# One core's diffusion layer: the last scan ahead of the early output projection, two blocks gathered in PSUM beside the norms, and the last five combinations in the rings of the others

## The chip, the core and the metric

The kernel runs on one core of one Trainium2 chip. Its work is done by TensorE (PE in the rows: matmuls; PEld is its loading of weights), VectorE (DVE), ScalarE (ACT) and GpSimd (POOL); SyncE (SP) issues most transfers. The metric is the device time of one execution in microseconds (us). The time before is the median of three runs. One more execution was recorded by the hardware profiler; its span runs from the first to the last recorded instruction.

## The reference

One layer of a diffusion backbone over 512 latent tokens of width 1024 with a context of 256. A token mixer (two groups of gated linear recurrences, four heads each, scanned in both directions), one output projection, a norm, and then a retrieval of experts:

```python
def reference(x, c, ctx, c_ctx, w_ada, ...):
    ...
    u_l = modulate(x, sh1_l, sc1_l) @ w_in[i]
    u_c = modulate(xc, sh1_c, sc1_c) @ w_in[i]
    mix_c, mix_l = token_mixer(u_c, u_l, rows, ...)
    x = layer_norm(ALPHA * x + g1_l * (mix_l @ w_out[i]), ln_gamma[i, 0], ln_beta[i, 0])
    ...
    y_l = peer(modulate(x, sh2_l, sc2_l), peer_w_query[i], peer_sub_keys[i], peer_u[i], peer_v[i])
    x = layer_norm(ALPHA * x + g2_l * y_l, ln_gamma[i, 1], ln_beta[i, 1])
...
def block(t):          # inside peer: 128 tokens
    q = (t @ w_query).reshape(PEER_BLOCK, PEER_HEADS, 2, PEER_DQ // 2)
    s1 = jnp.einsum('thd,nd->thn', q[:, :, 0], k1)
    s2 = jnp.einsum('thd,nd->thn', q[:, :, 1], k2)
    ...            # top 16 of each half, then top 16 of their sums: idx and weights g
    act = jax.nn.gelu(jnp.einsum('thkd,td->thk', expert_u[idx], t))
    return jnp.einsum('thk,thkd->td', (g * act), expert_v[idx])
```

`mix_l @ w_out` is a sum over eight heads of 128 columns; `sh1` to `g2` are six rows of 1024 numbers from a small matmul on `c`.

## The kernel before

The 512 tokens stand in four blocks of 128, the width of 1024 in two halves of 512 columns, since one PSUM bank holds 128 x 512 numbers. Most products are made in full precision by splitting each operand into a high and a low part: the high part is a copy by ACT, the low part a subtraction on DVE or POOL (`mTh`/`mTl`, `lasth`/`lastl`, `wq0h`/`wq0l`, `hh`/`hl`, `wqh`/`wql`, `uh`/`ul`, `vh`/`vl`, `ah`/`al`), and `mm3` (L139 to L141) makes three matmuls of it. An operand that is not split (an identity of plain float32) costs one longer matmul.

**The mixer's end.** The mixer works in six units; each is projected and then scanned, and the last unit ends head 3 of the eight. When all units are projected, a planner weaves two generators by their accumulated costs: the last scan and `out_proj_early` (L603), which sums seven heads of the output projection, all but the last one. For each block and half that is 21 matmuls in a PSUM bank `pe`; then DVE writes x times ALPHA plus that sum to SBUF (`part` for the first half, a free piece of `mT` for the second, L631). In all, four blocks of 42 matmuls. The matmul queue is in order, so the weave is fixed when the program is built. At the end of the scan: `po` (the last outputs), squares and a root, the gated `G`, four transposes `pyt` (L574), the copy `mT` (L579), and from it `lasth`. Rows of modulation (`prow`, L252) are made between.

**The output projection and the norms** (`out_proj`, L635). For each block, two halves `pout`, each the identity times the stored partial sum (L678) and three matmuls with the last head, in PSUM with two buffers. DVE takes statistics (L680), then the affine of the first norm (`x`, L134 and L135), statistics again (L119, L125), the affine of the modulation (`h`), then eight transposes on PE (`pht`, L702), the copy `hh` on ACT (L704) and the subtraction `hl` on DVE (L705). The first two query slabs multiply `hh`, `hl` in `first_queries`, two blocks at a time (48 matmuls of 256 columns, tile `pq`), and `pss` (L715) makes scores of them.

**PEER.** `Peer.run` makes the other fourteen query slabs (`query`, L886; the subtraction `wql` on POOL, L895) while DVE picks the top sixteen, builds gates, and then runs over 128 rows of 128 experts: `pH` multiplies `uh`/`ul` with the tokens, and `combine` adds the row of `v` to six PSUM banks `y` (three blocks of tokens, two halves, 18 matmuls a row). The fourth block is served by gathers on POOL and DVE into `yg`. The main loop's rings hold two buffers of `ah`/`al`, and a ring `vring` of the deeper rows opens when the last `pH` is done.

**The tail.** The last seven rows are kept back (`TAIL`): pools are closed and others opened, the row g2 is made (L1289 and the lines ahead of it), the norm's rows are loaded, and then the seven rows are combined one block and half after the other, so that the final norm (`finish`, L1137) of a block can stand beside the matmuls of the next.

## Time and profile before

| | |
|---|---|
| Time, median of 3 runs | 1796.12 us (1792.1 to 1796.97) |
| The profiled execution | 1791.8 us |
| Its span | 1789.9 us |
| Busy share of the span | PE 96%, PEld 83%, DVE 81%, ACT 46%, POOL 23% |
| Mean granted clock of TensorE | 0.985 of full speed |

Busy shares count an engine's instructions, and a matmul's end is modelled: two matmuls of 0.39 us whose starts stand 0.23 us apart overlap, so the pitch of the starts is what a matmul costs in a row of them. The chain that ended last is the path that sets the end. A wait in the rows is idle time of an engine, with the instruction that ended it.

### The profile page before, as it was taken

The page shows a single profiled execution, that of the slowest core. Times are in us where ns is not written, and L with a number is a line of the kernel's source. Part 1 is how long each engine was busy: PE and PEld are TensorE (multiplying, and loading weights), DVE is VectorE, ACT ScalarE, POOL GpSimd, SP SyncE. Part 2 cuts the span into 40 slices and gives each one's busy share as a digit, 9 for nine tenths or more (in the row PEclk, how much of TensorE's full clock was granted, in tenths as well). Part 3 has the DMA queues.
Part 4 walks back from the last instruction along what each step waited for, and adds up shares of the span by engine and source line. Part 5 has one row for each costly group of instructions (what it writes and reads, how often), then busy time and mean ns, then how long its engine had stood idle before and what let it go on. Part 6 is the DMA issues. An engine that isn't in the chain of part 4 may idle for free.

```text
span 1789.9 us, 28456 instructions
## 1 busy us (share of the span) xinstructions
PE 1720.3 (96%) x10485; PEld 1490.7 (83%) x10485; DVE 1456.1 (81%) x2914; ACT 831.2 (46%) x1417; POOL 409.3 (23%) x287
## 2 busy tenths in 40 slices
PE   7999999999879999999999999999999999999996
PEld 2788887877668899999998899999999998888885
DVE  6679879875689999999996878788788786867767
ACT  5477676654233345767674333333333333333332
POOL 0000000000013202128622545344344342111001
PEclk9999999989989999999999999999999999999998
DMA  8523535332232247898999999999999989998834
GB/s 298 181 86 124 171 96 168 98 128 99 86 117 83 67 130 271 302 325 306 330 320 358 337 336 368 317 320 335 315 314 335 316 306 320 364 323 281 276 111 172
DMA packets 174814, 429.02 MB, mean 240 GB/s; under 512 B 14993, under 2 KB 78801, under 8 KB 170578
## 3 DMA queue, kind: packets, MB, share of 16 engines
q1 hardware_dynamic: 137234, 290.87, 47.5%
q0 software_dynamic: 36864, 134.23, 21.4%
q10 hardware_dynamic: 576, 2.10, 0.3%
q8 instruction: 82, 1.34, 0.3%
q14 instruction: 58, 0.48, 0.1%
HBM read 378.38 MB, written 48.76 MB: 239 GB/s over the span
## 4 chain that ended last, share of the span: by engine, by line
PE 77%; DVE 10%; DMA 5%; issue 5%; ACT 2%; POOLq 0%; SPq 0%; POOL 0%; DVEq 0%; ACTq 0%
PE y L139 9%; PE y L141 9%; PE y L140 9%; PE pH L139 8%; PE pH L141 8%; PE pH L140 8%; PE pG L1025 3%; PE pc L139 2%; PE pc L140 2%; PE pc L141 2%; DMA wada<-in_w_ada_dram 2%; DMA vr<-in_v_dram 2%; PE pq L141 1%; PE pq L139 1%; PE pq L140 1%
## 5 line engine op out<-in xcount | busy, mean ns | idle before, releaser
L139 PE MATMUL pH<-hh,uh 128*128 128x384 f32 x1024 | 350.0, 342 | 1.0 <-ACT gels L1061 1.0
L141 PE MATMUL pH<-hh,ul 128*128 128x384 f32 x1024 | 347.7, 340 | 1.6 <-DVE ul L1048 1.6
L140 PE MATMUL pH<-hl,uh 128*128 128x384 f32 x1024 | 347.1, 339 | 0.0
L139 PE MATMUL y<-vh,ah 128*128 128x512 f32 x768 | 302.6, 396 | 7.1 <-ACT ah L1087 4.1
L140 PE MATMUL y<-vl,ah 128*128 128x512 f32 x768 | 302.2, 394 | 1.6 <-POOL vl L1048 1.3
L141 PE MATMUL y<-vh,al 128*128 128x512 f32 x768 | 301.4, 394 | 0.4 <-DVE al L1088 0.4
L1117 POOL DMA_INDIRECT erow<-in_u_dram,ix x128 | 185.0, 1445 | 371.4 <-DVE scr L1126 212.8
L1117 POOL DMA_INDIRECT erow<-in_v_dram,ix x128 | 184.0, 1437 | 333.2 <-DVE yg L1134 180.2
L1046 ACT ACTIVATE uh<-ur 128x1024 fp32r<-128x1024 f32 x128 | 135.5, 1059 | 249.5 <-PE pH L140 182.0
L1048 DVE TENSOR_TENSOR vl<-vr,vh 128x1024 fp32r<-128x1024 f32 x127 | 155.3, 1224 | 66.9 <-ACT vh L1046 66.7
L1087 ACT ACTIVATE ah<-gel 128x384 fp32r<-128x384 f32 x128 | 66.4, 524 | 291.8 <-issue 219.0
L139 PEld LDWEIGHTS pH<-hh,uh 128*128 128x128 f32 x1024 | 192.4, 188 | 3.8 <-ACT gels L1061 1.4
L140 PEld LDWEIGHTS pH<-hl,uh 128*128 128x128 f32 x1024 | 192.7, 188 | 2.7
L141 PEld LDWEIGHTS pH<-hh,ul 128*128 128x128 f32 x1024 | 192.3, 188 | 2.6 <-DVE ul L1048 2.4
L139 PEld LDWEIGHTS y<-vh,ah 128*128 128x128 f32 x768 | 144.6, 188 | 38.0 <-ACT ah L1087 4.7
L141 PEld LDWEIGHTS y<-vh,al 128*128 128x128 f32 x768 | 144.8, 188 | 34.8 <-DVE al L1088 0.8
L140 PEld LDWEIGHTS y<-vl,ah 128*128 128x128 f32 x768 | 145.0, 189 | 33.5 <-POOL vl L1048 1.8
L1048 DVE TENSOR_TENSOR ul<-ur,uh 128x1024 fp32r<-128x1024 f32 x128 | 156.0, 1219 | 17.5 <-PE pH L141 15.5
L1134 DVE SCALAR_TENSOR_TENSOR yg<-erow,act,yg 128x1024 f32<-128x1024 f32 x127 | 162.3, 1278 | 0.2
L1088 DVE TENSOR_TENSOR al<-gel,ah 128x384 fp32r<-128x384 f32 x128 | 70.7, 557 | 105.6 <-ACT ah L1087 104.4
L1126 DVE SCALAR_TENSOR_TENSOR scr<-erow,h 128x1024 bf16<-128x1024 f32 x128 | 155.9, 1218 | 0.0
L1046 ACT ACTIVATE vh<-vr 128x1024 fp32r<-128x1024 f32 x128 | 133.8, 1047 | 39.7 <-DMA vr<-in_v_dram 29.6
(340 smaller groups left out, 3122.3 us busy)
## 6 DMA issues: line engine op xcount, KB each, us to landing
ur<-in_uT_dram SPq DMA_DIRECT2D x128, 512.0 KB
vr<-in_v_dram SPq DMA_DIRECT2D x128, 512.0 KB
Gd<-stage SPq DMA_DIRECT2D x24, 1024.0 KB
Gn<-Gd SPq DMA_DIRECT2D x16, 1536.0 KB
wraw<-in_w_cf_dram SPq DMA_DIRECT2D x24, 512.0 KB
wada<-in_w_ada_dram SPq DMA_DIRECT2D x48, 256.0 KB
Hd<-gels SPq DMA_DIRECT2D x56, 192.0 KB
gel<-Hd SPq DMA_DIRECT2D x56, 192.0 KB
```

The costliest lines, as they stand in the source:

```text
L139: mm(out, lh, rh, start=start, stop=False)
L140: mm(out, lh, rl, start=False, stop=False)
L141: mm(out, ll, rh, start=False, stop=stop)
L1025: nc.tensor.matmul(p[:, t, :], o[:, q, 1, :, e], f[:, q, j, :, e], start=j == 0, stop=j == 2)
L1046: nc.scalar.activation(hi, raw, AF.Copy)
L1048: sub = eng.tensor_tensor(lo, raw, hi, op=OP.subtract)
L1087: nc.scalar.activation(ah, g, AF.Copy)
L1088: nc.vector.tensor_tensor(al, g, ah, op=OP.subtract)
L1117: nc.gpsimd.indirect_dma_start(out=e, out_offset=None, in_=a[src], in_offset=bass.IndirectOffsetOnAxis(ap=self.ix[:, j:j + 1], axis=0))
L1126: nc.vector.scalar_tensor_tensor(scr, e, 1.0, h2, op0=OP.mult, op1=OP.mult, accum_out=dots[:, j:j + 1])
L1134: nc.vector.scalar_tensor_tensor(y, e, act[:, j:j + 1], y, op0=OP.mult, op1=OP.add)
```

## The change

Four edits. First, the planner is gone: the whole of the last scan is emitted, and then `out_proj_early`, which does blocks 0 and 1 alone (`NB = 2`). Blocks 2 and 3 are gathered in two pairs of PSUM banks, `pl2` and `pl3`, in `late_block`, which is emitted behind the norm of block 0 (for block 2) and of block 1 (for block 3): x times ALPHA by a matmul with a scaled identity `aident`, then the seven heads, and later the last head in the same banks. So these two blocks have neither `part` nor the matmul that brings it back. To make room, the tile `po` of blocks 0 and 1 and of the first queries has one buffer for each half. Second, the split `wql` of query slab 2 goes from POOL to DVE. Third, `TAIL` is 5, `ah`/`al` have five buffers in the main loop, and the five last rows take `v` from the rings of the main loop; the rows of g2 and of the norm lie in a buffer of gates (`Gn`), and `finish` works in tiles of the ring `vr`. No pool is closed. Fourth, the loads of `w_g2` have one buffer.

```diff
@@ out_proj_early, with split_heads and project_heads taken out of it
+    def split_heads(self, g, sl):
+        mh, ml = (self.wo.tile([128, 4, 128], F32R, name=n, bufs=2)[:, :len(g)] for n in ("mTh", "mTl"))
+        m = self.mT[:, g[0]:g[-1] + 1, sl]
+        self.nc.scalar.activation(mh, m, AF.Copy)
+        self.nc.vector.tensor_tensor(ml, m, mh, op=OP.subtract)
+        return mh, ml
+
+    def project_heads(self, ps, g, m, first, last):
+        for p, (wh, wl) in zip(ps, self.w):
+            for i, k in enumerate(g):
+                self.mm3(p, m[0][:, i, :], m[1][:, i, :], wh[:, k, :], wl[:, k, :], first and i == 0, last and k == g[-1])
...
-        part = wo.tile([128, 4, 512], F32, name="part")
+        part = wo.tile([128, NB, 512], F32, name="part")
...
-        yield 0.05
-        for b in range(4):
+        for b in range(NB):
...
@@ out_proj
-        sh2 = self.mod_row(pool, ps, 1, "sh2", "po0")
+        sh2 = self.mod_row(pool, ps, 1, "sh2", "pht")
...
+        aid = self.wo.tile([128, 128], F32, name="aident")
+        nc.vector.tensor_scalar(aid, self.ident, ALPHA, None, op0=OP.mult)
+
+        banks = lambda n: [ps.tile([128, 512], F32, name=f"{n}{hf}", bufs=1) for hf in range(2)]
+        r3, r0, r2 = (banks(n) for n in ("pl3", "po", "pl2"))
+        rl = {0: r0, 2: r2, 3: r3}
+
+        def late_block(b):
+            sl = slice(b * 128, (b + 1) * 128)
+            for hf in range(2):
+                x = self.wo.tile([128, 512], F32, name="xe", bufs=2)
+                nc.sync.dma_start(x, a["x"][sl, hf * 512:(hf + 1) * 512])
+                nc.tensor.matmul(rl[b][hf], aid, x, start=True, stop=False)
+            for g in self.groups:
+                self.project_heads(rl[b], g, self.split_heads(g, sl), False, False)
...
-            r = [ps.tile([128, 512], F32, name=f"pout{hf}", tag=f"po{hf}") for hf in range(2)]
+            r = rl[b] if b in rl else banks("po")
             for hf, (wh, wl) in enumerate(self.w):
-                nc.tensor.matmul(r[hf], self.ident, self.parts[b, hf], start=True, stop=False)
+                if b < NB:
+                    nc.tensor.matmul(r[hf], self.ident, self.parts[b, hf], start=True, stop=False)
...
+            if b < NB:
+                late_block(b + NB)
@@ the mixer's end
-        early = [self.out_proj_early(seq[-1], pool(eps, "eps", space=PSUM, bufs=3))]
-        pe = ps
+        early = pool(eps, "eps", space=PSUM, bufs=3)
         while scan:
-            if early and pe < ps:
-                pe = advance(early, pe)
-            else:
-                ps = advance(scan, ps)
-        for e in early:
-            for _ in e:
-                pass
+            ps = advance(scan, ps)
+        self.out_proj_early(seq[-1], early)
@@ query
-        nc.gpsimd.tensor_tensor(wl, raw, wh, op=OP.subtract)
+        eng = nc.vector if j == 2 else nc.gpsimd
+        eng.tensor_tensor(wl, raw, wh, op=OP.subtract)
@@ finish and run
-    TAIL = 7
+    TAIL = 5
...
-        r = w.tile([128, D], F32, name="fin", bufs=2)
-        x1 = w.tile([128, D], F32, name="fx1", bufs=2)
+        x1, r = (ring.tile([128, 8, 128], F32, name="vr", bufs=4).rearrange("p k c -> p (k c)") for _ in range(2))
...
-                    ops = self.gated(m, w, w, 2, mark), v
+                    ops = self.gated(m, w, w, self.TAIL, mark), v
...
+                for c, m in enumerate(tail):
+                    mark = self.mark
+                    vs.append(self.rows(m, w, w, 2) if c < 2 else self.rows(m, vp, vp, 3, rbufs=4))
+                    acts.append(self.gated(m, w, w, self.TAIL, mark))
+
+                rows = w.tile([128, NG, self.GN, self.GT], F32, name="Gn", bufs=2)
...
```

The diff alone does not tell the order on the engines, which a scheduler sets. Three places follow. In these rows a line number of the changed kernel stands 3 higher than before for the small helpers (L139 is L142) and 23 higher in the loop over blocks (L678 is L701).

**The end of the scan, PE.** Before, `pe` (the early projection) is woven through the scan and ends ahead of the scan's last steps; `psc`, `po`, `pyt` are the scan's, `prow` a row of modulation, `pout` the first block of the output projection:

```order
L140 MATMUL pe<-wo_4340,mTh 128x512
L141 MATMUL pe<-wo_4339,mTl 128x512
L511 MATMUL psc<-arg 64x64 x8
L252 MATMUL prow<-ident,m_242 128x128 x8
L557 MATMUL po<-S,QT 128x128 x7
L560 MATMUL po<-V,A 128x128 x4
L574 MATMUL pyt<-ident,G 128x128 x4
L252 MATMUL prow<-ident,m_242 128x128 x8
L678 MATMUL pout_4913<-part,ident 128x512
L139 MATMUL pout_4913<-wo_4337,lasth 128x512
```

In the changed kernel the last transposes stand among the early projection's matmuls:

```order
L142 MATMUL pe<-wo_4591,mTh 128x512
L143 MATMUL pe<-wo_4592,mTh 128x512
L577 MATMUL pyt<-ident,G 128x128
L144 MATMUL pe<-wo_4591,mTl 128x512
L577 MATMUL pyt<-ident,G 128x128 x2
L142 MATMUL pe<-wo_4591,mTh 128x512
L577 MATMUL pyt<-ident,G 128x128
L143 MATMUL pe<-wo_4592,mTh 128x512
L144 MATMUL pe<-wo_4591,mTl 128x512
L142 MATMUL pe<-wo_4593,mTh 128x512
```

Behind these come eleven more `pe`, and then the row and the first block, now named `po`, with the first two matmuls of the late block 2 (`pl`):

```order
L144 MATMUL pe<-wo_4593,mTl 128x512
L255 MATMUL prow<-ident,m_242 128x128 x13
L701 MATMUL po_4798<-part,ident 128x512
L142 MATMUL po_4798<-wo_4591,lasth 128x512
L143 MATMUL po_4798<-wo_4592,lasth 128x512
L144 MATMUL po_4798<-wo_4591,lastl 128x512
L701 MATMUL po_4799<-mT,ident 128x512
L142 MATMUL po_4799<-wo_4593,lasth 128x512
L143 MATMUL po_4799<-wo_4594,lasth 128x512
L144 MATMUL po_4799<-wo_4593,lastl 128x512
L685 MATMUL pl_4800<-xe,aident 128x512
L685 MATMUL pl_4801<-xe,aident 128x512
```

From the point where the two orders part, 66 `pe` matmuls are left on PE where there were 150; fourteen of them stand behind the last `pyt`.

**Block 1 on PE.** Before, the first three blocks' `pout` stand one behind the other, then the transposes `pht` of block 0, then block 3:

```order
L678 MATMUL pout_5008<-mT,ident 128x512
L139 MATMUL pout_5008<-wo_4339,lasth 128x512
L140 MATMUL pout_5008<-wo_4340,lasth 128x512
L141 MATMUL pout_5008<-wo_4339,lastl 128x512
L702 MATMUL pht<-ident,h_4873 128x128 x8
L678 MATMUL pout_5056<-part,ident 128x512
L139 MATMUL pout_5056<-wo_4337,lasth 128x512
L140 MATMUL pout_5056<-wo_4338,lasth 128x512
L141 MATMUL pout_5056<-wo_4337,lastl 128x512
L678 MATMUL pout_5057<-mT,ident 128x512
```

In the changed kernel all 42 matmuls of block 2 (`pl_4800`, `pl_4801`) stand ahead of block 1 (`po_4904`, `po_4905`), with the transposes of block 0 in their midst, 29 behind the two `aident`; block 3 (`pl_4796`, `pl_4797`) follows in the same way, and then the last head of blocks 2 and 3:

```order
L144 MATMUL pl_4801<-wo_4593,mTl 128x512
L701 MATMUL po_4904<-part,ident 128x512
L142 MATMUL po_4904<-wo_4591,lasth 128x512
L143 MATMUL po_4904<-wo_4592,lasth 128x512
L144 MATMUL po_4904<-wo_4591,lastl 128x512
L701 MATMUL po_4905<-mT,ident 128x512
L142 MATMUL po_4905<-wo_4593,lasth 128x512
L143 MATMUL po_4905<-wo_4594,lasth 128x512
L144 MATMUL po_4905<-wo_4593,lastl 128x512
L685 MATMUL pl_4796<-xe,aident 128x512
L685 MATMUL pl_4797<-xe,aident 128x512
L142 MATMUL pl_4796<-wo_4591,mTh 128x512
```

The transposes of block 1 have 28 of block 3's matmuls ahead of them and 14 behind. Then come twelve matmuls of the last head, the 48 of the first queries, and the transposes of blocks 2 and 3.

**The norms on DVE.** Before, the blocks are interleaved: the affine and the statistics of one stand between those of another (`x_4879`, `h_4873` are block 0, `x_4880` is block 1):

```order
L680 BN_STATS sto<-pout_5007 128x6
L134 SCALAR_TENSOR_TENSOR h_4873<-x_4879,mvp,sc_4805 128x1024
L125 BN_AGGR mvo<-sto 128x2
L680 BN_STATS sto<-pout_5008 128x6
L135 SCALAR_TENSOR_TENSOR h_4873<-h_4873,rsp,sh_4887 128x1024
L134 SCALAR_TENSOR_TENSOR x_4880<-pout_4960,mvo,gam_4881 128x512
L134 SCALAR_TENSOR_TENSOR x_4880<-pout_4961,mvo,gam_4881 128x512
L135 SCALAR_TENSOR_TENSOR x_4880<-x_4880,rso,bet_4883 128x512
L705 TENSOR_TENSOR hl<-pht,hh 128x4x128
L135 SCALAR_TENSOR_TENSOR x_4880<-x_4880,rso,bet_4883 128x512
L705 TENSOR_TENSOR hl<-pht,hh 128x4x128
L119 BN_STATS stp<-x_4880 128x6 x2
```

In the changed kernel block 0 is gone through to its `hl`, and block 1 (`po_4904`, `x_4764`) begins behind it; two splits `mTl` of the late blocks stand between:

```order
L606 TENSOR_TENSOR mTl<-mT,mTh 128x384
L138 SCALAR_TENSOR_TENSOR h_4757<-h_4757,rsp,sh_4771 128x1024
L728 TENSOR_TENSOR hl<-pht,hh 128x4x128 x2
L606 TENSOR_TENSOR mTl<-mT,mTh 128x512
L703 BN_STATS sto<-po_4904 128x6
L703 BN_STATS sto<-po_4905 128x6
L128 BN_AGGR mvo<-sto 128x2
L137 SCALAR_TENSOR_TENSOR x_4764<-po_4904,mvo,gam_4765 128x512
L137 SCALAR_TENSOR_TENSOR x_4764<-po_4905,mvo,gam_4765 128x512
L138 SCALAR_TENSOR_TENSOR x_4764<-x_4764,rso,bet_4767 128x512 x2
L122 BN_STATS stp<-x_4764 128x6 x2
L128 BN_AGGR mvp<-stp 128x2
```

Blocks 2 and 3 are interleaved with each other behind that. The split `wql` of query slab 2 stands on DVE ahead of the first of the picks. In the main loop the order on PE is as it was; in the tail the row `prow` and then 90 `y` matmuls stand behind the last row, where there were 126.

## Rows read from the trace of the kernel before

**Rows 1.** The page: busy time of each engine with its share of the span and its count of instructions, and the chain that ended last, by engine.

```profile
PE 1720.3 (96%) x10485; PEld 1490.7 (83%) x10485; DVE 1456.1 (81%) x2914; ACT 831.2 (46%) x1417; POOL 409.3 (23%) x287
...
PE 77%; DVE 10%; DMA 5%; issue 5%; ACT 2%; POOLq 0%; SPq 0%; POOL 0%; DVEq 0%; ACTq 0%
```

**Rows 2.** The view by stretches: start and end in us, length, then busy us (and instructions) of PE, PEld, DVE, ACT and POOL, the granted TensorE clock, the DMA share and GB/s. From the top: the last scan with the early projection; the norms with the first two query slabs; the picks; the gates and the main loop; the tail.

```profile
419.20:471.90 52.70, 49.59 (x309) 40.55 (x307) 24.24 (x54) 14.55 (x24) 0.00 (x0) 0.97 0.23 73
471.90:522.70 50.80, 37.73 (x189) 29.64 (x188) 41.41 (x81) 17.63 (x40) 0.74 (x2) 0.86 0.25 93
522.70:622.00 99.30, 97.56 (x489) 82.36 (x490) 94.87 (x607) 31.20 (x44) 33.51 (x14) 1.00 0.25 76
622.00:1743.40 1121.40, 1112.98 (x6369) 1004.51 (x6368) 927.49 (x1424) 486.61 (x813) 368.98 (x256) 1.00 0.88 304
1743.40:1789.90 46.50, 32.73 (x143) 25.98 (x141) 34.08 (x50) 11.44 (x18) 4.71 (x1) 0.89 0.48 170
```

**Rows 3.** Groups of PE's instructions by line and shape in 419.2 to 471.9 us (count | busy us, mean ns of one | idle before). The first and the last of the three lines of a split product; the third group, of L140, has the same count.

```profile
L139 PE MATMUL pe<-wo,mTh 128*128 128x512 f32 x50 | 20.0, 403 | 0.0
...
L141 PE MATMUL pe<-wo,mTl 128*128 128x512 f32 x50 | 19.7, 394 | 0.0
```

**Rows 4.** PE's timeline (start us, busy us, engine, line, operation, out<-in, count, idle before it). The first two rows are eight starts apart; the third stands directly ahead of the output projection; the last two are the starts of two neighbouring halves of it.

```profile
429.17 0.40 PE L139 MATMUL pe<-wo,mTh 128*128 128x512 f32 x1
...
430.99 0.39 PE L141 MATMUL pe<-wo,mTl 128*128 128x512 f32 x1
...
468.49 3.61 PE L252 MATMUL prow<-ident,m 128*128 128x128 f32 x16 [0.69 <-ACT mT L579]
...
473.57 1.02 PE L678 MATMUL pout<-mT,ident 128*128 128x512 f32 x2
...
475.12 1.02 PE L678 MATMUL pout<-part,ident 128*128 128x512 f32 x2
```

**Rows 5.** What PE waited for between 380 and 520 us: the waiting tile and line, the engine and line that ended the wait, us in total, times, the longest.

```profile
PE pht L702 <- DVE h L135: 12.0, 3, 4.1
PE psc L511 <- DVE arg L539: 2.8, 2, 2.2
PE pyt L574 <- DVE G L569: 2.4, 1, 2.4
PE psc L511 <- ACT sq L521: 1.5, 1, 1.5
```

**Rows 6.** DVE's timeline over the last of the four norm blocks, from the first affine to the end of `h`, with the third block's `hl` in its midst, and the last `hl` behind it.

```profile
502.48 1.41 DVE L134 SCALAR_TENSOR_TENSOR x<-pout,mvo,gam 128x512 f32<-128x512 f32 x2
504.02 1.29 DVE L705 TENSOR_TENSOR hl<-pht,hh 128x512 fp32r<-128x512 f32 x2
505.23 1.41 DVE L135 SCALAR_TENSOR_TENSOR x<-x,rso,bet 128x512 f32<-128x512 f32 x2
...
509.44 1.41 DVE L135 SCALAR_TENSOR_TENSOR h<-h,rsp,sh 128x512 f32<-128x512 f32 x2
...
512.88 0.69 DVE L705 TENSOR_TENSOR hl<-pht,hh 128x512 fp32r<-128x512 f32 x1 [0.16 <-ACT hh L704]
```

**Rows 7.** PE's timeline from the last transposes of the norms to the first matmul of the third query slab that reads `wql`.

```profile
510.24 1.97 PE L702 MATMUL pht<-ident,h 128*128 128x128 f32 x8 [3.89 <-DVE h L135]
...
518.07 0.28 PE L141 MATMUL pq<-hh,wq0l 128*128 128x256 f32 x1
518.19 0.28 PE L139 MATMUL pq<-hh,wq0h 128*128 128x256 f32 x1
...
519.96 1.35 PE L715 MATMUL pss<-sk,q 128*128 128x128 f32 x8
...
525.17 0.50 PE L141 MATMUL pq<-hh,wql 128*128 128x512 f32 x1 [1.72 <-POOL wql L895]
```

**Rows 8.** Two of DVE's groups in 471.9 to 513.7 us (count | busy us, mean ns of one | idle before).

```profile
L680 DVE BATCH_NORM_STATS2 sto<-pout 128x6 f32<-128x512 f32 x8 | 5.3, 666 | 3.9 <-PE pout L141 3.9
...
L662 DVE TENSOR_TENSOR wq0l<-wq0r,wq0h 128x1024 fp32r<-128x1024 f32 x2 | 2.4, 1207 | 0.0
```

**Rows 9.** What PE waited for in the tail, 1743 to 1790 us.

```profile
PE y L139 <- ACT vh L1046: 3.1, 1, 3.1
PE y L140 <- POOL vl L1048: 1.3, 1, 1.3
```

**Rows 10.** PE's timeline around the tail: two matmuls of the main loop, fifteen starts apart; the row of g2; the first and the last combination of the tail.

```profile
1739.63 0.40 PE L141 MATMUL y<-vh,al 128*128 128x512 f32 x1
...
1743.13 0.40 PE L141 MATMUL y<-vh,al 128*128 128x512 f32 x1
1743.36 1.95 PE L252 MATMUL prow<-ident,m 128*128 128x128 f32 x16
1748.37 0.94 PE L139 MATMUL y<-vh,ah 128*128 128x512 f32 x2 [3.05 <-ACT vh L1046]
...
1780.44 0.39 PE L141 MATMUL y<-vh,al 128*128 128x512 f32 x1
```

**Rows 11.** DVE's timeline of the tail: the second half of the first finish, and the start of the last half and the last affine of the last finish.

```profile
1745.98 0.69 DVE L1146 TENSOR_TENSOR fin<-yg,g 128x512 f32<-128x512 f32 x1 [0.20 <-ACT g L254]
...
1781.45 0.67 DVE L1146 TENSOR_TENSOR fin<-y,g 128x512 f32<-128x512 f32 x1
...
1785.19 1.41 DVE L135 SCALAR_TENSOR_TENSOR fin<-fin,rsz,bet 128x512 f32<-128x512 f32 x2
```

More of the change, by code (lines that the diff above doesn't have):

```diff
@@ L26 @@
 LEVELS = (128, 64, 32, 16, 8, 4, 2)
+NB = 2
 NN = (1, 3, 2, 0)
@@ L602, in out_proj_early @@
         self.w = [[wo.tile([128, 8, 512], F32R, name=f"wo{hf}{i}") for i in range(2)] for hf in range(2)]
-        groups = [g for g in (range(0, last), range(last + 1, 8)) if g]
+        self.groups = groups = [g for g in (range(0, last), range(last + 1, 8)) if g]
         for ks in (slice(0, 4), slice(4, 8)):
@@ L1135, in fetched, with finish @@
             yield
-    def finish(self, b, y, w, rows, out):
+    def finish(self, b, y, w, ring, rows, out):
         nc = self.nc
         g2, gam, bet = rows
-        r = w.tile([128, D], F32, name="fin", bufs=2)
-        x1 = w.tile([128, D], F32, name="fx1", bufs=2)
+        x1, r = (ring.tile([128, 8, 128], F32, name="vr", bufs=4).rearrange("p k c -> p (k c)") for _ in range(2))
         nc.sync.dma_start(x1, self.n.x1d[b])
@@ L1287, in run @@
-                g2 = n.mod_row(fw, hps, 3, "g2", "pH")
-                gam = fw.tile([128, D], F32, name="gam2")
-                nc.sync.dma_start(gam, a["ln_g"][1:2].to_broadcast([128, D]))
-                bet = fw.tile([128, D], F32, name="bet2")
-                nc.sync.dma_start(bet, a["ln_b"][1:2].to_broadcast([128, D]))
-                nc.scalar.preload_act_table_set("natural_log_exp_and_others")
-                rows = (g2, gam, bet)
-                vs = []
-                for c, i in enumerate(seq[128 - self.TAIL:]):
-                    if c == 4:
-                        self.finish(3, (yg[:, :512], yg[:, 512:]), fw, rows, out)
-                    if c < 2:
-                        vs.append(self.rows(i, w, w, 2))
-                    else:
-                        vs.append(self.rows(i, fw, fw, self.TAIL - 2, c == 5, 3))
+                tail = seq[128 - self.TAIL:]
@@ L1302, in run @@
+                nc.sync.dma_start(rows[:, 1], a["ln_g"][1:2].to_broadcast([128, D]))
+                nc.sync.dma_start(rows[:, 2], a["ln_b"][1:2].to_broadcast([128, D]))
+                nc.scalar.preload_act_table_set("natural_log_exp_and_others")
+                rows = [rows[:, i] for i in range(3)]
+                self.finish(3, (yg[:, :512], yg[:, 512:]), w, vp, rows, out)
                 for b in range(ND):
                     for hf in range(2):
-                        for i, a_, v in zip(seq[128 - self.TAIL:], acts, vs):
+                        for i, a_, v in zip(tail, acts, vs):
@@ L1305, in run @@
                             self.combine(i, b, (a_, v), (hf,))
-                    self.finish(b, self.y[b], fw, rows, out)
+                    self.finish(b, self.y[b], w, vp, rows, out)
 def build(tc, a, out):
```

28 lines of the change are left out of this document (9 added, 19 removed).

## The prediction

> **What bounds the kernel now.** I read the page first, then the stretches, then PE's groups and waits in the two stretches that the change touches, and last the timelines of their ends. The reader is to see that PE is the bound: it is busy for 96% of the span and carries 77% of the chain that ended last [rows 1]. In the picks it is busy for 97.56 of 99.30 us and in the main loop for 1112.98 of 1121.40 [rows 2]; no PE work leaves those stretches but the last two rows, so nothing large is to be had there. Three stretches differ. The last scan with the early projection fills 52.70 us with 49.59 of PE, so time leaves it only if PE's work leaves it. In the norms PE has 37.73 us of work in 50.80 while DVE has 41.41: there PE waits for DVE, 12.0 us in three waits of `pht` for `h` [rows 5]. The tail has 32.73 in 46.50. The change takes PE work out of the first and puts it into the second, where PE idles.
>
> **The scan's stretch.** Of 150 `pe` matmuls (three groups of 50 [rows 3]), 66 stay, and 84 leave. Eight starts lie 430.99 - 429.17 = 1.82 us apart [rows 4], 0.2275 each: 84 x 0.2275 = 19.1 us. Of the idle 52.70 - 49.59 = 3.1 us, 2.4 is the wait of `pyt` for `G` [rows 5] and 0.69 that of the row for `mT` [rows 4]. In the new order `pe` matmuls stand before, between and behind the `pyt` (14 behind the last, 3.2 us), so both go: 3.1. The row that follows took 3.61 us behind the idle time [rows 4], the same row 1.95 in the tail [rows 10]; behind a busy PE I count the latter: 1.6. Against it stands a new wait. With fewer `pe` matmuls between them, the scan's own matmuls come sooner than its arguments; the waits seen around here are 2.8 and 1.5 for `psc` and 2.4 for `pyt` [rows 5], so the new idle time lies between 0 and their sum, 6.7. I take 2.4, one such wait, since `pe` matmuls are left between most of the scan's steps. The first block of the output projection then starts 19.1 + 3.1 + 1.6 - 2.4 = 21.4 us earlier, near 450.5.
>
> **The norms.** From the first `pout` (471.90) to `pss` (519.96 [rows 7]) they take 48.06 us. I walk through the new order with 0 at the first `po`. Two neighbouring halves start 1.55 us apart [rows 4]; less three matmuls of 0.2275, the identity costs 0.87. PE: block 0 to 3.1; two `aident` to 4.8; 29 late matmuls to 11.4; `pht` about 1.0 to 12.4 (half of the 1.97 that it took behind an idle PE [rows 7]); 13 more to 15.4; block 1 to 18.5; two `aident` and 28 matmuls to 26.6; `pht` to 27.6; 14 to 30.8; twelve with the last head to 33.5; the first queries, 48 at 0.12 (518.07 to 518.19 [rows 7]), to 39.2.
>
> DVE: from the first affine to the end of `h` a block took 502.48 to 510.85, less 505.23 - 504.02 for another's `hl`, 7.1 us [rows 6]; with one more statistics of 0.6 to 0.67 [rows 8] and an aggregate ahead of it, 7.9 behind its second half. Block 0's `h` ends at 3.1 + 7.9 = 11.0, in time for the `pht` at 11.4; its `hl` follow 2.0 to 3.3 us behind that start (510.24 to 513.57 in the old run [rows 6, 7]), by 13.9. Then DVE waits, since block 1 is not on PE before 15.4; its `h` ends at 18.5 + 7.9 = 26.4, its `hl` at 29.3. Block 2's first half ends at 31.5, and the two last blocks, interleaved, take 2 x 7.1 and four statistics and two aggregates, 17.2, and some small gaps: the last `h` is done near 49.1. From the last `h` to the end of the second queries was 519.96 - 510.85 = 9.1 [rows 6, 7]: 58.2. So the stage grows by 10.1. It was filled by DVE before; now DVE stands idle where a block waits for its place on PE. Bounds: 54 (48.06 plus the two waits of DVE, 3.1 for block 1 and 2.2 for block 2, with nothing else later than before) and 63 (each of the three places where PE's order and DVE's cross missed by 1.6, a half).
>
> The Trainium skill, Perfetto Trace Analysis, section Matmuls, speaks against this part: independent groups of matmuls should rotate through PSUM banks, so that one is evacuated while the next is made. Here `po` falls from two buffers to one. The rows on `po`: its last reader is the first affine, 3.1 + 0.7 + 0.2 + 1.3 = 5.3 in my walk, and the order has block 1 on PE at 15.4, so the wait is none and the sum stands; without the late matmuls between, the rule would cost 5.3 - 3.1 = 2.2 at this place. No run so far shows it.
>
> The middle gives 21.4 - 10.1 = 11.3 us.
>
> **The split of slab 2.** PE waits 1.72 us for POOL's `wql` [rows 7]; DVE does the like split in 1.21 [rows 8]. DVE does it ahead of its first pick, and DVE is busy for 94.87 of 99.30 us there [rows 2]. PE may gain up to 1.7, the picks may come up to 3 us later, but DVE's 99.30 - 94.87 = 4.4 us of idle time there can take them up. I take 0; ends -1.7 and +3.
>
> **The main loop and the tail.** The further buffers of `ah` change no order on PE, which is full: 0. The loads of `w_g2` with one buffer: DVE may wait, PE has no wait there: 0, up to +1. Tail before: 1743.36 to 1789.9 is 46.5 us. After: two rows go to the main loop, 36 matmuls at (1743.13 - 1739.63)/15 = 0.233 [rows 10], 8.4; the row 1.95; 90 matmuls at 0.2275, 20.5. PE is done at 30.85, where it took 1780.44 + 0.23 - 1743.36 = 37.3. The difference, 6.4, is the wait of 3.05 for `vh` and 1.3 for POOL's `vl` [rows 9], and slow matmuls behind the idle time (granted clock 0.89 in this stretch [rows 2]): the five rows' `v` now lie in rings that are free before the loop ends, and POOL has no split. But DVE had 37 us for four finishes and has 30.9. One takes 5.15 from 1781.45 to 1786.60 for half of the products and the affines [rows 11], and three products of 0.69 for the other half, 7.2. The first began near 1745.3, 1.9 behind the row's start, and the span ended 3.3 behind the last affine. DVE alone: 8.4 + 1.9 + 28.8 + 3.3 = 42.4; PE alone: 30.85 + 9.2 (1780.67 to 1789.9) = 40.1. I take 41.05, in the middle with a tendency to PE, whose matmuls are in time for all but the last finish: gain 5.5, ends 4.1 and 6.4, or 2.5 if a wait of 3.05 for `vh` is left.
>
> **Sum.** 11.3 + 5.5 = 16.8 us. The profiled execution took 1791.8, 1.9 more than its span, and lies at the lower end of the runs shown; on it the sum gives 1775.0, on the median of 1796.12 it gives 1779.3. I predict 1777, between the two.
>
> **Rivals.** (1) The scan's chain of ACT and DVE, not PE, sets the stretch: the new idle time is 6.7 and not 2.4, and the gain 12.5: 1781. For it: the waits of rows 5; against it: DVE has 24.24 and ACT 14.55 us of work in 52.70 [rows 2], and the early projection's share of it leaves as well. (2) The tail stays: DVE's four finishes set the end and a wait for `vh` is left; gain 11.3 to 13: 1782. For it: DVE has 34.08 of 46.50 there [rows 2]. (3) Slower: with one `po` and the late matmuls in an in-order queue, the blocks come one after the other. Each is 3.1 on PE, 7.9 on DVE and 3.3 to `hl`, 14.3; four are 57; the late work, 84 x 0.2275 + 4 x 0.87 = 22.6, is hidden by none of it where a split `mTl` comes late on DVE, and six more for the last queries make 86. The stage would be 28 longer than I take: 1805. This decides from a stage of 48.06 + 21.4 + 5.5 = 75 us on. For it: in the new order blocks 0 and 1 are no longer interleaved on DVE; against it: two of the four are, and the late matmuls stand beside block 0's and 1's norms, not behind them. The rule of the Trainium skill named above is what this would bear out. (4) That the change moves nothing, since the work is only reordered: PE's idle time of 3.1, 13.1 and 4.4 us in the three stretches is real, [rows 2, 9], so this needs two of the others together: some 5 us of gain left, 1789.
>
> **How the numbers follow.** Forecast 0.66 (gain 11 to 24); rival 1 0.14; rival 2 0.10; rival 3 0.06; rival 4 0.04. The forecast's bounds: 4.2 more from the stage and 2.4 from the wait give 1770, and 1768 on the profiled run's scale; a stage of 63 with a wait of 6.7 gives 1786, and 1788 with a late pick. That holds rivals 1 and 2. A difference under 0.3%, 5.4 us, can't be told from none. Faster by more than that: 0.66 + 0.14 + 0.10 less 0.04 for their pairs, 0.86; within 0.3%: 0.04 of rival 4 and 0.03 of such pairs, 0.07; slower: rival 3 and a little more, 0.07.
>
> **What would show it.** In the changed kernel's profile the first `po` starts between 446 and 453, and PE's idle time ahead of it is 1 to 4 us; the stage to `pss` is 54 to 63 us long, with DVE idle for block 1's statistics and PE's waits for `h` under 10; PE's wait for `wql` of slab 2 is gone; the tail has no wait for `vh` or POOL, and its last `y` stands about 9 us before the end. I am wrong if the first `po` stays near 460, if `pss` comes behind 515, or if the tail from the row of g2 keeps more than 36 us.

## The result and the profile after

The changed kernel took 1771.61 us in the median of four runs (1770.05 to 1782.29), the kernel before 1794.18 in four (1792.1 to 1796.97): a ratio of 0.9886, interval 0.9844 to 0.9928. The forecast was 1777 with a range of 1768 to 1788. The profiled execution took 1771.05 us, its span 1768.9, 21.0 under that of before; the sum had 16.8.

The stretches of the changed kernel that answer to [rows 2] (start, end, length, then busy us and instructions of PE, PEld, DVE, ACT, POOL, the granted clock, the DMA share, GB/s): the scan from 417.0, the norms up to the last scores, the picks, the gates and the main loop, and the tail.

```profile
417.00:448.27 31.27, 31.03 (x239) 24.89 (x239) 21.69 (x49) 15.30 (x28) 0.00 (x0) 1.00 0.29 98
448.27:506.23 57.96, 51.51 (x263) 41.55 (x262) 40.22 (x61) 15.43 (x37) 0.00 (x0) 0.91 0.27 91
...
1736.09:1768.90 32.81, 22.82 (x107) 18.50 (x105) 27.89 (x46) 5.71 (x13) 0.00 (x0) 0.89 0.30 108
```

In the scan's stretch PE is now idle for 31.27 - 31.03 = 0.24 us, where it was for 3.1 [rows 2]. The norms are longer, 57.96 us against 48.06, and hold 51.51 us of PE's work instead of 35.7 (the 37.73 of [rows 2] are of a stretch that ends 2.7 us later). The tail is 32.81 us long.

What PE waited for between 380 and 520 us, against [rows 5] (waiting tile, what ended the wait, us in total, times, the longest):

```profile
PE pht L725 <- DVE h L138: 5.5, 2, 3.2
PE psc L514 <- DVE arg L542: 2.9, 2, 2.2
PE psc L514 <- ACT sq L524: 1.5, 1, 1.5
...
PE pq L144 <- DVE wql L915: 0.5, 1, 0.5
```

The wait of 2.4 for `G` is gone, the waits of `pht` fell from 12.0 to 5.5, and the wait for `wql` is 0.5, on DVE, instead of 1.72 on POOL. The `psc` waits stand as they did: they lie ahead of the point where the orders part.

PE's timeline at the places of [rows 4, 7]: the row ahead of the output projection, the first block, block 0's transposes, block 1, and the last scores (start, busy, line, out<-in).

```profile
445.37 3.06 PE L255 MATMUL prow<-ident,m 128*128 128x128 f32 x26
448.27 1.02 PE L701 MATMUL po<-part,ident 128*128 128x512 f32 x2
...
459.77 1.09 PE L725 MATMUL pht<-ident,h 128*128 128x128 f32 x8
...
463.67 1.02 PE L701 MATMUL po<-part,ident 128*128 128x512 f32 x2
...
506.23 1.35 PE L740 MATMUL pss<-sk,q 128*128 128x128 f32 x8
```

Block 1 starts 463.67 - 448.27 = 15.4 us behind block 0, as the walk had it, and the last scores 57.96 behind it.

DVE's timeline between block 0 and block 2 (idle time and what ended it in brackets):

```profile
458.43 1.28 DVE L138 SCALAR_TENSOR_TENSOR h<-h,rsp,sh 128x1024 f32<-128x1024 f32 x1
461.15 1.29 DVE L728 TENSOR_TENSOR hl<-pht,hh 128x512 fp32r<-128x512 f32 x2 [1.44 <-ACT hh L727]
464.30 0.69 DVE L606 TENSOR_TENSOR mTl<-mT,mTh 128x512 fp32r<-128x512 f32 x1 [1.86 <-ACT mTh L605]
465.41 0.70 DVE L703 BATCH_NORM_STATS2 sto<-po 128x6 f32<-128x512 f32 x1 [0.42 <-PE po L144]
...
480.00 2.10 DVE L703 BATCH_NORM_STATS2 sto<-pl 128x6 f32<-128x512 f32 x3 [2.45 <-PE pl L144]
```

DVE has ended block 0's `h` by 459.7 and comes to block 1's statistics at 465.4; between them are 3.7 us of waits and three instructions. Before block 2 it waits 2.45 again.

To compare executions I take five marks from each trace: the last matmul of the mixer's projections, the first of the output projection, the last scores `pss` of the norms, the row of g2 ahead of the tail, and the end of the span. Each number is a difference of two starts in us; the table has all the kernels of this study.

| Kernel | projections to first output block | norms | to the row of g2 | tail | span |
|---|---|---|---|---|---|
| before | 84.49 | 48.06 | 1223.40 | 46.54 | 1789.9 |
| changed | 58.94 | 57.96 | 1229.86 | 32.81 | 1768.9 |
| changed, again | 58.92 | 57.92 | 1237.90 | 32.85 | 1772.5 |
| tail alone | 82.27 | 47.74 | 1233.23 | 32.86 | 1783.9 |
| scan and late blocks alone | 59.11 | 57.99 | 1224.76 | 46.04 | 1773.5 |
| order alone | 81.03 | 45.86 | 1227.55 | 46.89 | 1788.7 |
| late blocks in pieces | 58.92 | 52.12 | 1230.59 | 32.86 | 1762.8 |
| block 2 ahead of block 3 | 59.02 | 49.83 | 1236.02 | 32.81 | 1764.1 |
| the same, again | 61.25 | 49.82 | 1232.22 | 32.88 | 1761.9 |
| slab 2 on POOL | 61.22 | 58.05 | 1238.18 | 32.86 | 1776.4 |
| four rows kept back | 62.51 | 58.81 | 1238.23 | 31.38 | 1780.8 |
| three blocks early, two buffers | 68.95 | 48.11 | 1237.43 | 32.82 | 1774.5 |
| three blocks early, one buffer | 71.95 | 49.45 | 1231.03 | 32.88 | 1771.7 |

Norms and tail repeat from execution to execution of one order, mostly within 0.1 us and at most within 0.9; the first and the third column do not, which the last section takes up.

### The profile page after: what moved, and what is told of

It is laid out like the page before. It is cut to its first block, busy times and chain, and to the rows that moved or that the text cites. A ratio compares the mean times of both kernels' runs of the same rounds, so it can differ in the third digit from the quotient of the medians.

```text
span 1768.9 us, 28164 instructions
## 1 busy us (share of the span) xinstructions
PE 1711.5 (97%) x10485; PEld 1484.2 (84%) x10485; DVE 1448.7 (82%) x2913; ACT 833.1 (47%) x1417; POOL 406.4 (23%) x285
## 5 line engine op out<-in xcount | busy, mean ns | idle before, releaser
L142 PE MATMUL pH<-hh,uh 128*128 128x384 f32 x1024 | 350.1, 342 | 1.0 <-ACT gels L1081 1.0
L142 PE MATMUL y<-vh,ah 128*128 128x512 f32 x768 | 302.7, 395 | 4.1 <-ACT ah L1107 4.1
L1137 POOL DMA_INDIRECT erow<-in_u_dram,ix x128 | 188.8, 1475 | 371.7 <-DVE scr L1146 213.8
L142 PEld LDWEIGHTS pH<-hh,uh 128*128 128x128 f32 x1024 | 192.4, 188 | 3.8 <-ACT gels L1081 1.4
L142 PEld LDWEIGHTS y<-vh,ah 128*128 128x128 f32 x768 | 144.5, 188 | 34.9 <-ACT ah L1107 4.7
L1068 DVE TENSOR_TENSOR ul<-ur,uh 128x1024 fp32r<-128x1024 f32 x128 | 155.7, 1217 | 15.7 <-PE pH L144 13.6
L142 PE MATMUL pc<-hTh,wh 128*128 128x512 f32 (+1 forms) x304 | 109.6, 361 | 0.4 <-ACT V L398 0.4
```

The source lines that it names most:

```text
L142: mm(out, lh, rh, start=start, stop=False)
L1068: sub = eng.tensor_tensor(lo, raw, hi, op=OP.subtract)
L1137: nc.gpsimd.indirect_dma_start(out=e, out_offset=None, in_=a[src], in_offset=bass.IndirectOffsetOnAxis(ap=self.ix[:, j:j + 1], axis=0))
```

## The experiments

**The tail alone.** The kernel before with the hunks on `TAIL`, `gated`, `finish`, `run` and `wg2`.

```diff
-    TAIL = 7
+    TAIL = 5
...
-                    ops = self.gated(m, w, w, 2, mark), v
+                    ops = self.gated(m, w, w, self.TAIL, mark), v
...
```

> The kernel before with the tail alone changed (five rows kept back, rings of the main loop, single buffer of w_g2). My account: the first output projection stays at 471.9 us and the norms at 48.1; from the row of g2 to the end it is 32.8 us instead of 46.5, and the main loop is 8.4 longer, so the span is 5.3 shorter, near 1784.6. Rival, that the tail's gain needs the mixer's change or that DVE's finishes give it back: 0 to 2 shorter.

Measured: ratio 0.9976 (0.9954 to 0.9998), span 1783.9. The tail is 32.86 us and two rows, 8.4 us, have gone into the main loop, so by the marks the tail's gain stands on its own: 46.54 - 32.86 - 8.4 = 5.3. The medians of this set lie 2.8 us apart, and the interval, 0.4 to 8.2 us, holds the 5.3. The same run served as a second picture of the scan as it was before. What PE waited for from 417 us to its first output block:

```profile
PE pyt L574 <- DVE G L569: 2.4, 1, 2.4
PE prow L252 <- ACT mT L579: 0.7, 1, 0.7
```

These are the two waits that the change removed, and they are all of PE's waits there.

**The scan and the late blocks alone.** The kernel before with the hunks on the planner, `out_proj_early` and `out_proj`.

> The kernel before with the scan, the early projection and the late blocks alone changed. My account: first block of the output projection at 448.3, the last scores at 506.2, so 13.7 us earlier than before; the wait for POOL's split of slab 2 stays at 1.7; the tail stays at 46.5; span near 1776. Rival, that the split of slab 2 on DVE is worth what the middle gained beyond the sum (1.9): then the picks' stretch is as before and the span is 1776; if it is not the split, the picks' stretch is 1 to 2 shorter here too, and the span 1774.5.

Measured: ratio 0.9942 (0.9917 to 0.9966), span 1773.5. The stretches repeat those of the changed kernel (59.11 and 57.99), the tail that of before, and the wait for POOL's split is 1.71. From the projections to the last scores it is 117.10 us where the tail's run, of the old order, has 130.01: the middle gives 12.9 us. The time to the row of g2 is 1.4 longer than before, not shorter; so this comparison does not tell where the 1.9 us come from by which that time beat the two rows' 8.4 in the changed kernel; the split's wait explains 1.2 of them. In the medians of one set the tail and the middle alone gain 2.8 and 10.8 us, 13.6 together, where the whole change gains 22.6 beside its own runs of the kernel before. The marks give 5.3 and 12.9, and the split 1.2; why the two medians have less is not shown.

**The order alone.** The scan emitted first, all four blocks early, no late block.

```diff
-            if early and pe < ps:
-                pe = advance(early, pe)
-            else:
-                ps = advance(scan, ps)
+            ps = advance(scan, ps)
```

> The kernel before with the last scan emitted ahead of the early projection, all four blocks still early, no late blocks. My account: the work of PE in the stretch stays, only its idle time of 3.1 and the slow row's 1.6 can go, so the first block starts 2 to 5 us earlier (467 to 470), and the norms stay at 48: span 2 to 5 shorter. Rival, that the order and not the work moved out of the stretch gives the gain: the first block starts before 460 and the span is 10 or more shorter.

Measured: ratio 0.9991 (0.9972 to 1.001), the first block 81.03 us behind the projections: 3.5 under before, 1.2 under the tail's run, which has the old order. The 3.5 is the like comparison: near 400 us the granted clock was at half for 13.7 us in this execution and in that of before, and for 6.8 in the tail's run (last section). The norms were 45.86, some 2 us shorter, but the scores of the next slab took 17.37 us instead of 15.79, 3.4 of them at half clock. What the order gives by itself is some 4 us by these marks, and the median does not tell it from nothing. Of the gain of 23 in the scan's stretch the order has 3.5, and the 84 matmuls the rest, some 20 (with 42 of them out the first block stands at 68.95, in the last experiment).

**The late blocks in pieces.** The changed kernel; three heads of block 2 come ahead of block 1, so that block 1 waits on PE for 18 late matmuls and not for 42.

```diff
             for g in self.groups:
                 self.project_heads(rl[b], g, self.split_heads(g, sl), False, False)
+                yield
...
-            if b < NB:
-                late_block(b + NB)
+            for n in LATE[b]:
+                next(late.setdefault(n, late_block(n)))
...
+LATE = {0: (2,), 1: (2, 3), 2: (3,), 3: ()}
```

> The changed kernel with each late block emitted in two pieces: three heads of block 2 before block 1, four heads of it and three of block 3 behind block 1, the rest behind block 2. My account, that the norms are 10 longer because block 1 waits on PE behind 42 late matmuls while DVE idles: block 1 starts 9 to 10 us behind block 0 instead of 15.4, DVE's idle time among the four norms falls from about 9.5 to under 5, and the stage from 58.0 to 50 to 54; span 1761 to 1765. Rival, that the single pair of banks for blocks 0 and 1 or DVE's own work sets the stage: the stage stays at 57 to 58 with a wait of block 1 for block 0's affine or of the late blocks elsewhere; span 1768.

Measured: ratio 0.9841 (0.9808 to 0.9874), norms 52.12 instead of 57.96. DVE's waits among the norms, changed kernel first (the view of waits on DVE, from the first output block to the last scores):

```profile
DVE hl L728 <- ACT hh L727: 4.4, 5, 1.4
DVE sto L703 <- PE pl L144: 2.4, 1, 2.4
DVE sto L703 <- PE po L144: 2.1, 3, 0.9
DVE mTl L606 <- ACT mTh L605: 1.9, 1, 1.9
...
```

```profile
...
DVE hl L732 <- ACT hh L731: 3.6, 4, 1.4
DVE sto L707 <- PE pl L145: 1.3, 1, 1.3
DVE sto L707 <- PE po L145: 0.9, 1, 0.9
...
```

Of 4.4 + 2.4 + 2.1 + 1.9 = 10.8 us of waits 3.6 + 1.3 + 0.9 = 5.8 are left (under 5 were expected), 5.0 less, and the stage is 5.8 shorter. The stage cut in two at the end of the last `h` tells the rest; the columns are those of [rows 2], DVE the third, the clock behind POOL. First the kernel before, then the changed one, then the pieces:

```profile
471.90:510.85 38.95, 26.60 (x124) 19.49 (x124) 36.88 (x58) 11.09 (x29) 0.00 (x0) 0.89 0.32 121
510.85:519.96 9.11, 9.11 (x56) 8.64 (x55) 1.87 (x4) 4.42 (x6) 0.00 (x0) 0.69 0.01 2
```

```profile
448.27:497.70 49.43, 42.98 (x209) 33.49 (x208) 38.84 (x59) 11.01 (x31) 0.00 (x0) 0.94 0.31 107
497.70:506.23 8.53, 8.53 (x56) 8.06 (x55) 1.38 (x2) 4.42 (x6) 0.00 (x0) 0.73 0.00 0
```

```profile
447.23:491.71 44.48, 42.31 (x209) 32.90 (x208) 38.87 (x59) 10.93 (x31) 0.00 (x0) 0.99 0.31 119
491.71:499.35 7.64, 7.64 (x55) 7.17 (x54) 1.39 (x3) 4.42 (x6) 0.00 (x0) 0.82 0.00 0
```

Up to the last `h` the changed kernel takes 10.5 us more than before. DVE's idle time there is 49.43 - 38.84 = 10.6 instead of 2.1, which is 8.5 of it; the other 2.0 are busy time, with instructions that follow each other with less overlap. So most of the growth is DVE waiting for PE's order. The pieces take 5.0 us of that idle time away. The other 0.9 lies behind the last `h`, where PE does the same work with 0.82 of its clock instead of 0.73.

**Block 2 ahead of block 3.** The same with `LATE = {0: (2,), 1: (2,), 2: (3, 3), 3: ()}`.

> As the kernel with the late blocks in pieces, but block 2 is finished ahead of block 3: the rest of block 2 and its last head behind block 1, all of block 3 after that. My account: DVE's wait of 1.3 for block 2's last head goes, since its banks are ready some 6 us earlier on PE, and block 3 is ready when DVE comes to it: stage from the first projection to the last scores 49 to 52 (52.1 with the first order), span 1760 to 1763. Rival, that block 3's banks, now behind everything, are late instead: stage 52 to 54.

Measured: ratio 0.9854 (0.9821 to 0.9886), norms 49.83; the wait of 1.3 for `pl` is gone. The same two stretches:

```profile
445.44:488.47 43.03, 42.10 (x210) 32.58 (x208) 38.58 (x59) 10.70 (x31) 0.00 (x0) 1.00 0.31 112
488.47:495.27 6.80, 6.48 (x53) 6.05 (x53) 1.39 (x3) 4.43 (x6) 0.00 (x0) 1.00 0.17 70
```

Of the 8.1 us under the changed kernel 6.4 lie ahead of the end of the last `h`, where 4.5 us of DVE's idle time are left, and 1.7 behind it, where PE now has its full clock (2.4 GHz). In the changed kernel PE waits 3.2 and 2.3 us for `h`, and between these two waits its clock falls to half (1.2 GHz) and stays there for 10.3 us. Here its longest wait is 0.9, and the clock does not fall. The span was 1764.1 all the same, since the time to the row of g2 was 1236.02, six more than in the changed kernel. Whether this was the kernel's doing or the execution's had to be asked again, with the changed kernel beside it on one chip:

> The changed kernel once more, beside the next one on the same chip. My account: 20 to 23 us under the kernel before in the median; stage from the first projection to the last scores 58.0. Single executions scatter by up to 11 us where a gather of POOL takes 32 us instead of 7; if that is chance, its share of executions is the same here and in the kernel with pieces.

> The kernel with block 2 finished ahead of block 3, once more, on the same chip as the changed kernel. My account: stage 49.8 instead of 58.0 and nothing else moved, so 8 us under the changed kernel in executions without the long gather, 28 to 31 under the kernel before. Rival, that what the stage gains comes back in the main loop (its first profile had 1236.0 from the scores to the row of g2, the changed kernel 1229.9): then that time is 1236 here again, without a gather of 32 us, and the gain 2.

Measured: the changed kernel 1774.67 us in the median of six (1772.52 to 1785.37), ratio 0.9872 (0.9846 to 0.9897); the one with block 2 first 1769.97 in five (1762.54 to 1771.09), ratio 0.9824 (0.9801 to 0.9846). The norms were 57.92 and 49.82, 8.1 apart as expected; the time to the row of g2 was 1237.90 in the changed kernel this time and 1232.22 in the other, the reverse of the first pair. So that column belongs to the execution, and the rival falls. The medians lie 4.7 apart, the lowest runs 10.0; the 8.1 of the trace lies between. This version is faster than both kernels: each of its five executions is shorter than each of the six of the changed kernel.

**The split of slab 2 back on POOL.**

```diff
-        eng = nc.vector if j == 2 else nc.gpsimd
-        eng.tensor_tensor(wl, raw, wh, op=OP.subtract)
+        nc.gpsimd.tensor_tensor(wl, raw, wh, op=OP.subtract)
```

> The changed kernel with the split of query slab 2 back on POOL. My account: PE's wait for it is 1.7 instead of 0.5 and the next scores come 1.2 later; nothing else moves, span 1.2 longer. Rival, that the 1.9 us by which the picks and the main loop beat the sum come from elsewhere: the time from the last scores of the norms to the row of g2 stays near 1229.9.

Measured, from one profiled execution: 1778.18 us, with a time to the row of g2 of 1238.18, 8.3 over the first profile of the changed kernel, where 1.2 was expected, and 0.3 over its second. Both this execution and that second one have a long gather of POOL (last section). This scatter hides 1.2 us, so the time decides nothing. The rows at the place do:

```profile
PE pq L144 <- POOL wql L914: 1.7, 1, 1.7
```

against 0.54 in the changed kernel: 1.2 us. From the last scores of the norms to those of slab 2 it is 14.6 us in all eight traces with the split on DVE, 15.8 in three with it on POOL, and 17.4 in two, this one and the order alone, where the clock was at half for 3.4 us of it. So the wait is worth 1.2 us; these two executions lost 2.8 at this place, and none of the eight has that fall of the clock. What DVE pays for it, 1.22 us ahead of its picks, shows in no wait of PE there.

**Four rows kept back.** `TAIL = 4` in the changed kernel.

> The changed kernel with four rows kept back instead of five. Theory that DVE's four finishes set the tail's end (they run without a gap from 2.9 us behind the row of g2): the row of g2 comes 4.2 later, the tail from there stays at 32.8, the span is 4.2 longer, near 1773. Rival, that PE sets it: the tail is 4.1 shorter and the span stays at 1769.

Measured: ratio 0.991 (0.9879 to 0.9941), the tail 31.38 us, between the two. DVE's timeline of this tail, and PE's last combination:

```profile
1751.14 0.69 DVE L1165 TENSOR_TENSOR vr<-yg,Gn 128x512 f32<-128x512 f32 x1 [0.60 <-ACT Gn L257]
...
1776.10 1.41 DVE L138 SCALAR_TENSOR_TENSOR vr<-vr,rsz,Gn 128x512 f32<-128x512 f32 x2
```

```profile
1767.58 0.40 PE L144 MATMUL y<-vh,al 128*128 128x512 f32 x1
```

PE is done at 1767.8; DVE runs from 1751.14 to 1777.51 without an idle time, 26.4 us, and the span ends 3.3 behind it. The finishes set this tail. In the changed kernel they run from 1739.04 to 1765.59, 26.55:

```profile
1737.43 1.22 DVE L1068 TENSOR_TENSOR vl<-vr,vh 128x1024 fp32r<-128x1024 f32 x1 [2.04 <-ACT vh L1066]
...
1739.04 1.29 DVE L1165 TENSOR_TENSOR vr<-yg,Gn 128x512 f32<-128x512 f32 x2
...
1760.44 0.68 DVE L1165 TENSOR_TENSOR vr<-y,Gn 128x512 f32<-128x512 f32 x1
...
1764.18 1.41 DVE L138 SCALAR_TENSOR_TENSOR vr<-vr,rsz,Gn 128x512 f32<-128x512 f32 x2
```

They begin 2.95 behind the row instead of 1.72, because the last row's `vl` stands ahead of them, which waits 2.04 for `vh`. So DVE sets both tails, and the fourth row's 4.2 us come back by 1.4 only.

**Three blocks early, with two buffers and with one.** `NB = 3`, block 3 alone late and emitted behind block 1; the freed banks give `po` its second buffer, or stay empty.

```diff
-NB = 2
+NB = 3
+PO = 2
...
-            if b < NB:
-                late_block(b + NB)
+            if b == 1:
+                late_block(3)
```

> The changed kernel with three blocks early and only block 3 late, emitted behind block 1, and two buffers for the tile of blocks 0 to 2. My account: 24 more of the early matmuls per half stay ahead, 42 x 0.2275 = 9.6, so the first block starts 9 to 10 us later than in the changed kernel (68 to 69 us behind the last projection instead of 58.9), and the stage is 47 to 50, as before the change, since blocks 0 and 1 follow each other: span 1768 to 1771. Rival: the late work costs the stage its 10 us wherever it is put: stage 55 or more, span 1775.

> As the kernel with three early blocks, but with one buffer instead of two for the tile of blocks 0 to 2. Rule that the groups must rotate through banks: block 1 waits for block 0's first affine, 5.3 us behind block 0's start instead of 3.1, and the stage is 2 or more longer than 48.1. My account: PE fills the wait with block 3's late matmuls and DVE has block 0 to work on, so the stage is 48 to 49.

Measured, from one profiled execution each: with two buffers the first block 68.95 us behind the projections, the norms 48.11, as before the change; with one, the norms 49.45. PE's timeline with one buffer at block 0, block 1 and the first queries, which read the same tile:

```profile
458.34 1.02 PE L701 MATMUL po<-part,ident 128*128 128x512 f32 x2
...
463.42 1.13 PE L701 MATMUL po<-part,ident 128*128 128x512 f32 x2
...
484.52 0.35 PE L143 MATMUL po<-hh,wq0h 128*128 128x256 f32 x1 [2.08 <-DVE x L138]
```

The first is what the account says: the 42 matmuls cost 10.0 us ahead of the norms, and the norms without a crossing are 9.9 shorter, as short as they were. Late work in the changed kernel's order gave back among the norms what the second late block had saved ahead of them. With one buffer the first block comes 3.0 us later, but that is the clock near 400 us again, at half for 17.1 us against 6.8 with two. In the norms the result lies between the two expectations. Block 1 starts 463.42 - 458.34 = 5.1 us behind block 0, when block 0's affine has read its banks, and PE has filled the time with two `aident` and a late matmul: no wait stands there. The wait comes later, 2.08 us of the first queries for block 2's affine, which has read the same banks only then. The Trainium skill (Perfetto Trace Analysis, section Matmuls) has independent groups of matmuls rotate through PSUM banks. The trace agrees so far that groups which share one pair wait here, at another place than the 2.2 of the prediction. The stage is 1.3 longer, but how much of that is the buffer's is not shown: the first scores come no later for the wait (35.3 us behind the first block, 35.6 with two buffers), and 0.8 of the 1.3 lies behind the last `h`, where the granted clock was 0.67 against 0.75. In the changed kernel the banks of blocks 2 and 3 are their own, and no such wait stands in PE's view.

## Why the prediction was right

**The scan's stretch: right, one term too large.** The order, the 84 matmuls, the two waits and the slow row went as worked out: 23.8. The step that failed is the new wait, for which I took one `psc` wait of 2.4: PE is idle for 0.24 us. The scan's arguments are made while the `pe` matmuls that are left run. The first block came at 448.27, 23.6 earlier, against 21.4. Measured from the end of the projections it is 84.49 - 58.94 = 25.6, but part of it is the execution's: in the same piece of program the clock was granted at half for 13.7 us in that profile and for 6.8 in the tail's run (same order, 82.27) and in the changed kernel (rows in the last section). Against that run the change is worth 23.3.

**The norms: right in size and cause.** 58.2 foreseen, 57.96 measured, block 1 at 15.4 both times. The end of the last `h` was foreseen at 49.1 and came at 49.4. That this is DVE waiting for its block on PE, and not the single pair of banks, was argued then and is shown by the kernels in pieces: the same banks and the same work, with the late matmuls cut so that block 1 comes sooner, took 5.8 off, and the better order 8.1. The last term fits in part by luck: the 9.1 us from the last `h` to the scores were taken whole from the old run, where PE had 0.69 of its clock. The prediction has no word on the clock there; it fell again, to 0.73, and the term was 8.5. With the full clock of the better order it is 6.8. (The lower bound of 54 is 53.4 by its own terms; nothing hangs on it.)

**The split of slab 2: the wrong value between the bounds.** I took 0; the wait fell from 1.72 to 0.54, 1.2.

**The tail: right in size, in part by luck.** 41.05 foreseen with the two rows in it, 32.81 + 8.4 = 41.2 measured. PE waits for nothing in it, where [rows 9, 10] had 3.05 and 1.3. But the value in the middle, with a tendency to PE, hid that DVE alone sets the end, which the run with four rows shows. The sum for DVE alone was 42.4: the four finishes took 26.55 us and not 28.8, and began 2.95 behind the row and not 1.9. These two errors come to 1.2, and the middle happened to lie 1.35 under that bound.

**The sum.** 16.8 foreseen and 21.0 measured in the two profiled executions: 25.6 less 9.9 in the middle, 5.3 in the tail, 1.9 between them, and 1.9 lost in the start, whose code is the same. Of the 4.2 that I had too little, the wait of 2.2 and the split's 1.2 are mine; 2.2 of the clock, the 1.9 of the start and what the main loop scattered are the execution's.

**The rivals.** The scan's chain as the bound (1) would have shown PE idle by 6.7: it is 0.24. Of the tail's rival (2) the first half is so, DVE's finishes set the end; the wait for `vh` that is left stands on DVE (2.04), none on PE, and the tail gains 5.3 all the same. The serial one (3) needed a stage of 75, and it took 58; its place, block 1 behind the late matmuls, is where the 10 us lie. That the order alone moves nothing (4) is nearly so, as the kernel with the order alone shows, but the change takes work out too. Of the signs named, PE's idle time ahead of the first block was to be 1 to 4 us, and the wait for slab 2's `wql` was to be gone; 0.24 and 0.54 were measured.

## What to carry to other kernels

Work of an engine that bounds one stage can be moved to a stage where this engine waits, and the price is what it puts in front of the other engine: list for each piece that waits in the second stage what now stands ahead of it in the in-order queue, and cut the moved work so that the next piece comes before the waiting engine is idle (here 18 matmuls ahead of block 1 instead of 42: 5.8 us, and 8.1 with block 2 finished ahead of block 3). Walk both queues against each other with durations of the old trace; that gave the stage to 0.3 us, while the terms taken as a middle of two bounds were the ones that missed. A duration of the old trace holds the clock of its place, though: ask whether the new order leaves the waits behind which the clock fell. And where executions scatter by more than the term in question, read the term at its own place in the trace, and compare places with the same granted clock.

## What the runs showed of the hardware

One execution of the same program differs from the next by up to 13 us (1772.5 and 1785.4 in the changed kernel on one chip), and the traces show two places where it comes from. On POOL, one gather out of the 256 sometimes takes very long. In the changed kernel's second profile, against the same instructions in the first:

```profile
823.59 4.35 POOL L1137 DMA_INDIRECT erow<-in_u_dram,ix  x1 [0.66 <-DVE yg L1154]
828.60 26.86 POOL L1137 DMA_INDIRECT erow<-in_u_dram,ix  x1 [0.66 <-DVE yg L1154]
```

```profile
827.52 4.36 POOL L1137 DMA_INDIRECT erow<-in_u_dram,ix  x1 [0.65 <-DVE yg L1154]
832.53 7.63 POOL L1137 DMA_INDIRECT erow<-in_u_dram,ix  x1 [0.65 <-DVE yg L1154]
```

26.86 us instead of 7.63. DVE then stood waiting for the gathered rows, and PE for DVE:

```profile
DVE scr L1146 <- DMA erow<-in_u_dram,ix: 9.1, 2, 4.8
```

```profile
871.83 0.40 PE L1045 MATMUL pG<-ohg,oh 128*128 128x128 bf16 x2 [7.52 <-DVE ohg L1033]
```

and from the midst of these 7.52 us of idle time on PE had half its clock, 1.2 GHz, for 10.3 us (here the stretch of 5 us from 870; the columns as above):

```profile
870.00:875.00 5.00, 3.17 (x11) 3.18 (x12) 5.00 (x12) 0.24 (x1) 1.78 (x1) 0.50 1.02 405
```

The first matmul of `y` then stands 466.1 us behind the last scores of the norms, where it was 455.9. A gather of 23 to 32 us stands in the traces of five of the thirteen executions listed, in three different orders of the norms. All five are among the seven taken on one chip, and none among the four taken on another; why it happens is open. The second such place is near 400 us, where the two executions of one order differ in the clock that was granted at the same point of the program:

```profile
402.40:407.40 5.00, 5.00 (x24) 4.78 (x24) 2.31 (x6) 2.72 (x8) 0.00 (x0) 0.51 1.01 416
```

```profile
402.80:407.80 5.00, 4.70 (x31) 3.87 (x30) 4.57 (x10) 5.00 (x13) 0.00 (x0) 1.00 1.02 419
```

0.51 against 1.00 in a stretch of full DMA traffic (first before, then the tail alone). In all thirteen traces PE waits here 2.2 us for the scan's arguments, and its clock falls to half around the end of this wait. It falls 1.4 to 1.8 us behind it in seven traces and stays down for 6.8 us; 0.3 to 0.8 behind it in four, for 13.7; at the end or 0.6 ahead of it in two, for 17.1. This is worth 2.2 to 3.5 us: in the first column of the table the changed order of the scan has 58.9 to 59.1 with 6.8 us at half clock, 61.2 with 13.7 and 62.5 with 17.1. Why it falls sooner in one execution than in another is open.
